# Values and gates of three row groups as seven half-block products

## Chip, cores and metric

The kernel runs on one core of a Trainium2 chip. The metric is the device time of one execution in microseconds; lower is better. The engines of the core that matter here are PE (TensorE, the matrix unit, with its weight loads shown as PEld), DVE (VectorE), ACT (ScalarE), POOL (GpSimd) and SP (SyncE, which here issues every DMA from one queue, in order).

## What is computed

The input x has 2048 rows of 1024 float32 values. It passes a retention layer and then a sliding-window attention layer; the change lies in the retention layer alone:

```python
def retention_layer(x, g_norm, w_in, w_out, sin, cos):
    proj = rmsnorm(x, g_norm) @ w_in            # 1024 -> 1024 + 1024 + 2048 + 2048
    q, k, v, gate = jnp.split(proj, [...])
    q = theta_shift(q.reshape(b, s, 4, 256), sin, cos)
    k = theta_shift(k.reshape(b, s, 4, 256), sin, cos)
    v = v.reshape(b, s, 4, 512)
    o = rms(retention(q, k, v))                 # chunks of 128 rows, a 256x512 state per head
    o = o.reshape(b, s, 2048) * silu(gate)
    return x + o @ w_out
```

Inside `retention` each chunk computes `scores @ v` plus `q @ state`, and then updates the state with `k.T @ v`.

## The kernel before

Rows are cut into 4 groups of 512 (`T`), and a group is worked through head by head: 4 groups x 4 heads give 16 units `u`, with `(g, h) = units[u]`. Every product in 32-bit precision is made of three fast ones: each operand is split into a rounded high part (`hi`, a cast on ACT) and the rest (`lo`, a subtraction on DVE), and PE computes hi-hi, hi-lo and lo-hi into the same PSUM bank.

For a unit, `main(u)` computes three projections with `proj` (L119): queries and keys together (L297), values (L325), gates (L332). Each goes over the 1024 inputs in 8 k-tiles of 128. `wload` (L100) fetches the weights in pieces of two k-tiles (128x1024, 512 KB) into one of three buffers of the tag `raw` (L105), casts them on ACT (L114) and subtracts on DVE (L116) into `whi` and `wlo`, three buffers each. A piece serves 24 matmuls (2 k-tiles x 4 PSUM banks x 3). The four banks come from the pool `pp`, which has four buffers in all, so the next projection writes a bank when the evacuation of the last one has read it. x is split once per group into `xhi`, `xlo` (L255, L256); the row scale of the norm is applied at the evacuation of values (L319, L320) and gates (L329). `row_stats` (L152) computes that scale.

`ret(u)` (L335) is the retention of one unit in four chunks; its PSUM banks come from another pool (`rr`, four buffers). The state `S32` stays in SBUF for each of the four heads. `out_a(u)` (L442) multiplies with the unit's rows of the output weights, again through `proj` (96 matmuls), and adds into the residual (L449). The order is laid down by the loop at L479: `drive` emits `main(u + 1)` and `ret(u)` interleaved, two steps of `main` per chunk, and then `out_a(u)`. A planner then orders each engine's instructions by priority and by its own estimate of when each is ready, so instructions of neighbouring steps mix; the retention has priority.

After the last unit, `prep_b0` (L438) loads the first x tiles of the second layer (phase B) while the last output projection runs; the last unit's output tiles `ohi`, `olo` take buffers of the x tiles (L350).

## Time and profile before

| | us |
|---|---|
| median of 3 runs (lowest, highest) | 2559.8 (2559.3, 2562.02) |
| profiled execution, its own time | 2558.99 |
| its span, first to last instruction | 2557.2 |
| PE busy | 2512.2 (98%) |
| DVE busy | 1495.7 (58%) |
| ACT busy | 1015.9 (40%) |

The busy time of an engine is the union of its instructions' times. PE's matmuls overlap each other in the pipeline, so the length of one matmul in the trace (about 0.39 us at 512 columns) is longer than the distance from one start to the next. The retention layer (phase A) covers about the first 1710 us of the span, the attention layer the rest.

### The profile page before, as it was taken

The page shows a single profiled execution, that of the slowest core. Times are in us where ns is not written, and L with a number is a line of the kernel's source. Part 1 is how long each engine was busy: PE and PEld are TensorE (multiplying, and loading weights), DVE is VectorE, ACT ScalarE, POOL GpSimd, SP SyncE. Part 2 cuts the span into 40 slices and gives each one's busy share as a digit, 9 for nine tenths or more (in the row PEclk, how much of TensorE's full clock was granted, in tenths as well). Part 3 has the DMA queues.
Part 4 walks back from the last instruction along what each step waited for, and adds up shares of the span by engine and source line. Part 5 has one row for each costly group of instructions (what it writes and reads, how often), then busy time and mean ns, then how long its engine had stood idle before and what let it go on. Part 6 is the DMA issues. An engine that isn't in the chain of part 4 may idle for free.

```text
span 2557.2 us, 31659 instructions
## 1 busy us (share of the span) xinstructions
PE 2512.2 (98%) x12098; PEld 2045.6 (80%) x12098; DVE 1495.7 (58%) x2653; ACT 1015.9 (40%) x1859; POOL 485.2 (19%) x429
## 2 busy tenths in 40 slices
PE   8999999999999999999999999989999999999998
PEld 7888888888888888888888888868777777777887
DVE  5445456454455554545545455467876677677766
ACT  4332333342333334223333332334544455454553
POOL 0000000110000021000011000041425454363360
PEclk9999999999999999999999999999999999999999
DMA  5242232422223243222323222237332352433333
GB/s 190 75 162 87 83 103 95 161 97 85 83 83 116 78 148 111 79 90 84 112 94 129 90 76 86 83 124 248 108 117 86 124 169 67 140 132 99 132 100 107
DMA packets 92501, 283.32 MB, mean 111 GB/s; under 512 B 11019, under 2 KB 17340, under 8 KB 92348
## 3 DMA queue, kind: packets, MB, share of 16 engines
q1 hardware_dynamic: 92348, 281.29, 32.9%
q8 instruction: 95, 1.56, 0.3%
q14 instruction: 58, 0.48, 0.1%
HBM read 245.58 MB, written 38.82 MB: 111 GB/s over the span
## 4 chain that ended last, share of the span: by engine, by line
PE 91%; DVE 4%; DMA 2%; issue 2%; ACT 1%; POOL 1%; SPq 0%; POOLq 0%; ACTq 0%; DVEq 0%
PE pp_ao L136 4%; PE pp_ao L138 4%; PE pp_ao L137 4%; PE o_t L670 2%; PE s_t L633 2%; PE pp_bo L136 2%; PE pp_bo L138 2%; PE pp_bo L137 2%; PE pT_t L654 2%; PE sc_r L356 1%; PE ot_r L427 1%; PE dl_r L393 1%; PE dl_r L394 1%; PE o_r L401 1%; PE o_r L403 1%
## 5 line engine op out<-in xcount | busy, mean ns | idle before, releaser
L94 POOL TENSOR_SCALAR r_o_r<-sso_r,es_a 128x1 f32<-128x1 f32 x64 | 31.2, 488 | 1260.3 <-ACT jo_r L421 1260.3
L136 PE MATMUL pp_ao<-ohi_r,whi_ao 128*128 128x512 f32 x512 | 203.3, 401 | 0.0
L137 PE MATMUL pp_ao<-olo_r,whi_ao 128*128 128x512 f32 x512 | 203.2, 397 | 0.0
L138 PE MATMUL pp_ao<-ohi_r,wlo_ao 128*128 128x512 f32 x512 | 199.5, 398 | 0.0
L116 DVE TENSOR_TENSOR wlo_ao<-raw_ao,whi_ao 128x1024 fp32r<-128x1024 f32 x64 | 78.4, 1224 | 199.7 <-ACT whi_ao L114 199.4
L644 ACT ACTIVATE P_t<-P_t,nm_t 128x256 f32<-128x256 f32 (+1 forms) x256 | 127.6, 499 | 143.6 <-DVE nm_t L636 142.9
L114 ACT CAST whi_ao<-raw_ao 128x1024 fp32r<-128x1024 f32 x64 | 67.1, 1048 | 184.9 <-PE pp_ao L137 49.6
L636 DVE CUSTOM_DVE_ANT_0 P_t<-s_t,bias,nsnk 128x256 f32<-128x256 f32 (+1 forms) x256 | 115.2, 469 | 34.8 <-PE s_t L633 34.0
L473 ACT CAST Shi_r<-S 128x512 fp32r<-128x512 f32 x120 | 70.3, 618 | 119.9 <-PE o_r L403 69.7
L137 PEld LDWEIGHTS pp_ao<-olo_r,whi_ao 128*128 128x128 f32 x512 | 96.9, 189 | 22.9 <-issue 0.2
L138 PEld LDWEIGHTS pp_ao<-ohi_r,wlo_ao 128*128 128x128 f32 x512 | 96.7, 189 | 23.0
L136 PEld LDWEIGHTS pp_ao<-ohi_r,whi_ao 128*128 128x128 f32 x512 | 96.8, 189 | 22.4 <-issue 0.2
L414 DVE SCALAR_TENSOR_TENSOR S<-S,dl_r 128x512 f32<-128x512 f32 x112 | 73.5, 682 | 65.5 <-PE dl_r L395 65.3
L633 PEld LDWEIGHTS s_t<-kst,qst_b 128*128 128x128 f32 x512 | 83.1, 193 | 30.6 <-DVE nm_t L636 7.6
L633 PE MATMUL s_t<-kst,qst_b 128*128 128x256 f32 (+1 forms) x512 | 101.1, 298 | 6.2 <-DVE nm_t L636 4.7
L474 DVE TENSOR_TENSOR Slo_r<-S,Shi_r 128x512 fp32r<-128x512 f32 x120 | 78.1, 686 | 38.7 <-ACT Shi_r L473 38.3
L650 DVE TENSOR_SCALAR P_t<-P_t,den_t 128x256 f32<-128x256 f32 (+1 forms) x256 | 99.4, 451 | 1.9
L136 PE MATMUL pp_bo<-ohi_t,whi_bo 128*128 128x512 f32 x224 | 89.0, 402 | 3.6 <-DVE gate_b L597 3.6
L137 PE MATMUL pp_bo<-olo_t,whi_bo 128*128 128x512 f32 x224 | 88.3, 394 | 0.0
L116 POOL TENSOR_TENSOR wlo_bo<-raw_bo,whi_bo 128x1024 fp32r<-128x1024 f32 x28 | 70.7, 2528 | 87.0 <-ACT whi_bo L114 64.8
L138 PE MATMUL pp_bo<-ohi_t,wlo_bo 128*128 128x512 f32 x224 | 86.3, 394 | 0.0
L424 DVE SCALAR_TENSOR_TENSOR gate_a<-o_r,r_o_r,gate_a 128x512 f32<-128x512 f32 x64 | 48.0, 750 | 55.0 <-POOL r_o_r L95 43.6
(867 smaller groups left out, 7292.0 us busy)
## 6 DMA issues: line engine op xcount, KB each, us to landing
raw_ao<-in_wo_a SPq DMA_DIRECT2D x64, 512.0 KB, 3.3
res<-xmid SPq DMA_DIRECT2D x56, 256.0 KB, 3.0
raw_bo<-in_wo_b SPq DMA_DIRECT2D x28, 512.0 KB, 3.3
xin<-in_x SPq DMA_DIRECT2D x16, 512.0 KB, 3.4
xraw_b<-xmid SPq DMA_DIRECT2D x16, 512.0 KB, 3.5
xmid<-res SPq DMA_DIRECT2D x32, 256.0 KB, 2.9
xraw_a<-in_x_t SPq DMA_DIRECT2D x12, 512.0 KB, 3.3
x_r<-in_x_t SPq DMA_DIRECT2D x12, 512.0 KB, 5.3
```

Of the source, the lines that this page charges most:

```text
L114: nc.scalar.copy(hi, raw)
L116: eng.tensor_tensor(lo, raw, hi.bitcast(F32), op=ALU.subtract)
L136: nc.tensor.matmul(o, hi[:, kk, sl], xh, start=st, stop=False)
L137: nc.tensor.matmul(o, hi[:, kk, sl], xl, start=False, stop=False)
L138: nc.tensor.matmul(o, lo[:, kk, sl], xh, start=False, stop=sp)
L414: nc.vector.scalar_tensor_tensor(S32[h][:, d, :], S32[h][:, d, :], gamC[h], dl[d], op0=ALU.mult, op1=ALU.add)
L473: nc.scalar.copy(hi, S32[h][:, d, :])
L474: nc.vector.tensor_tensor(lo, S32[h][:, d, :], hi.bitcast(F32), op=ALU.subtract)
L633: nc.tensor.matmul(o, qst[m][:, h, :], kst[:, kv * 2 + hl, kb + b0 : kb + 2, :], start=hl == 0, stop=hl == 1)
L636: nc.vector.tensor_tensor_reduce(out=pt[:, j, :w], in0=o, in1=bias[:, kv * GQ + h, b0 * P :], scale=-1.0, scalar=nsv[:, h : h + 1], op0=AL ...
L644: nc.scalar.activation(pt[:, j, :w], pt[:, j, :w], AF.Exp, scale=-1.0, bias=nm[:, c : c + 1], accum_out=den[:, c : c + 1])
L650: nc.vector.tensor_scalar_mul(pt[:, j, :w], pt[:, j, :w], den[:, c : c + 1])
```

## The change

For the row groups 1 to 3 (units 4 to 15; group 0 is `PLAIN`) values and gates are computed together as one product of 512 rows x 1024 inputs with 1024 x 1024 weights (values and gates side by side), cut into halves in each direction and computed by seven products of halves (256 rows x 512 inputs x 512 columns) in Winograd's form, where the direct way takes eight. It needs four sums of row halves (S1 to S4) and four sums of weight halves (T1 to T4). Both are computed on DVE from pieces loaded for that purpose and stored in DRAM: the weight sums in units 1, 3, 4 and 5 (one head each), the row sums and the scaled rows in units 2, 6 and 10 (for the next group), step by step through the list `behind`. The rows are scaled by the norm's row scale there, so no scale is applied to the gates at evacuation.

In `strassen`, products 0, 2, 4 and 5 accumulate in two banks of the tag `a`, one on top of the other; products 1, 3 and 6 in two banks of the tag `b`. ACT copies the sum in `a` out after products 0, 2 and 4, and DVE adds a bank of `b` to such a copy for three of the four quadrants. The next group's rows and sums are loaded from DRAM while the last head of a group runs its products (`after`). Every weight piece now serves 12 matmuls. The number of `main` steps per retention chunk goes from 2 to 3 in these units.

Queries and keys are loaded as separate pieces of four k-tiles of 256 columns. `q`, `k`, the key splits and several short tiles have one buffer, the state is stored to DRAM after each unit and loaded for the next head into one buffer, and the last unit's output tiles take buffers of the row sums. The DMA queue's scratch size is set to 1024.

The diff, cut to its core:

```diff
+RAW = 3
+PLAIN = 4
+SX = ("S2", "S3", "S1", "S4")
+ST = ("T2", "T3", "T1", "T4")
...
-    xtp = ctx.enter_context(tc.tile_pool(name="xtp", bufs=2))
+    xtp = ctx.enter_context(tc.tile_pool(name="xtp", bufs=1))
-    pp = ctx.enter_context(tc.tile_pool(name="pp", bufs=4, space=bass.MemoryType.PSUM))
+    pp = ctx.enter_context(tc.tile_pool(name="pp", bufs=2, space=bass.MemoryType.PSUM))
+    def pbank(tag, name):
+        return pp.tile([P, 512], F32, tag=tag, name=name)
...
     def xt_tiles(name):
+        return [[xtp.tile([P, 2, T], F32R, tag=f"x{hl}{j}", name=f"x{hl}_{name}_{j}") for j in range(4)]
+                for hl in ("hi", "lo")]
...
-        S32 = [cst.tile([P, 2, DV], F32, name=f"S{h}") for h in range(RH)]
+        S_d = [dram.tile([P, 2, DV], F32, name=f"Sd{h}") for h in range(RH)]
+        behind = []
+        def step():
+            if behind and next(behind[0], "end") == "end":
+                behind.pop(0)
+        def stp(name):
+            return p1.tile([P, T], F32, tag="st", bufs=6, name=name)
+        def short(name):
+            return p1.tile([P, 512], F32, tag="r", bufs=4, name=name)
...
+        def stage_rows(g):
+            for m in range(MT):
+                nc.vector.tensor_scalar_mul(dg[:, m * P : (m + 1) * P], ident, r[:, m : m + 1])
+            rp = bank(f"rpx_{g}")
+            nc.tensor.matmul(rp, ones, dg, start=True, stop=True)
+            nc.vector.tensor_copy(rb, rp)
+            yield
+            for k in range(KT // 2):
+                t = [stp(f"xst_{g}_{k}_{j}") for j in range(2)]
+                for j in range(2):
+                    kk = k + KT // 2 * j
+                    nc.sync.dma_start(t[j], x_t[g, kk // 2, :, kk % 2, :])
+                yield
+                for j in range(2):
+                    kk = k + KT // 2 * j
+                    nc.vector.scalar_tensor_tensor(t[j], t[j], ags[:, kk : kk + 1], rb, op0=ALU.mult, op1=ALU.mult)
+                a11, a21, a12, a22 = t[0][:, :H], t[0][:, H:], t[1][:, :H], t[1][:, H:]
+                nc.vector.tensor_tensor(s1, a21, a22, op=ALU.add)
+                nc.vector.tensor_tensor(s2, s1, a11, op=ALU.subtract)
+                nc.vector.tensor_tensor(s3, a11, a21, op=ALU.subtract)
+                nc.vector.tensor_tensor(s4, a12, s2, op=ALU.subtract)
+                for j in range(2):
+                    nc.sync.dma_start(d[kk // 2][:, kk % 2, :], t[j])
+                for n, v in zip(SX, (s2, s3, s1, s4)):
+                    nc.sync.dma_start(ds[n][:, k, :], v)
+                yield
+        def load_part(hi, lo, src, name):
+            raw = wp.tile(list(hi.shape), F32, tag="raw", bufs=RAW, name=f"xb_{name}")
+            nc.sync.dma_start(raw, src)
+            nc.scalar.copy(hi, raw)
+            nc.vector.tensor_tensor(lo, raw, hi.bitcast(F32), op=ALU.subtract)
...
+        def stage_sums(h):
+            for c in range(4):
+                b = [[stp(f"b{h}_{c}_{i}{j}") for j in range(2)] for i in range(2)]
+                for i in range(2):
+                    for j in range(2):
+                        nc.sync.dma_start(b[i][j], vg[i, j, c // 2, :, c % 2, :])
+                yield
+                nc.vector.tensor_tensor(b22, b22, b12, op=ALU.subtract)
+                nc.vector.tensor_tensor(b12, b12, b11, op=ALU.subtract)
+                nc.vector.tensor_tensor(b11, b22, b11, op=ALU.add)
+                nc.vector.tensor_tensor(b21, b21, b11, op=ALU.subtract)
+                for t, dt in zip((b11, b22, b12, b21), d):
+                    nc.sync.dma_start(dt[c // 2, :, c % 2, :], t)
+                yield
+        def strassen(n, src, xt, evac, after):
+            a = [pbank("a", f"pp_{n}a{f}") for f in range(2)]
+            def result(i, j, part=None, bk=None):
+                for f in range(2):
+                    if part is None:
+                        evac(i, j, f, a[f])
+                        continue
+                    nc.vector.tensor_tensor(r[part][f], r[part][f], bk[f], op=ALU.add)
+                    evac(i, j, f, r[part][f])
+            for p in range(7):
+                if p in (1, 3):
+                    b = [pbank("b", f"pp_{n}b{p}{f}") for f in range(2)]
+                dst = b if p in (1, 3, 6) else a
+                for i, w in enumerate(src(p)):
+                    hi, lo = wload(w, 512, f"{n}_{p}{i}")
+                    for kk in range(2):
...
+                        start, stop = k == 0 and p in (0, 1, 3), k == KT // 2 - 1
+                        for f in range(2):
+                            nc.tensor.matmul(dst[f], xh[:, sl], hi[:, kk, :], start=start, stop=False, **kw)
+                            nc.tensor.matmul(dst[f], xh[:, sl], lo[:, kk, :], start=False, stop=False, **kw)
+                            nc.tensor.matmul(dst[f], xl[:, sl], hi[:, kk, :], start=False, stop=stop, **kw)
+                    if i == 0:
+                        step()
+                        yield
+                if p in (0, 2, 4):
+                    r[p] = [short(f"r_{n}_{p}{f}") for f in range(2)]
+                    for f in range(2):
+                        nc.scalar.copy(r[p][f], a[f])
+                if p == 1:
+                    result(0, 0, 0, b)
+                elif p == 4:
+                    result(1, 1, 4, b)
+                elif p == 5:
+                    result(0, 1)
+                elif p == 6:
+                    result(1, 0, 2, b)
+                after(p)
+                step()
+                yield
...
-            q = p2.tile([P, 2, T], F32, tag="q", name=f"q_{n}")
-            k = p2.tile([P, 2, T], F32, tag="k", name=f"k_{n}")
+            q = p1.tile([P, 2, T], F32, tag="q", name=f"q_{n}")
+            k = p1.tile([P, 2, T], F32, tag="k", name=f"k_{n}")
...
+            yield from project_qk(u, xt, q, k, load_trig if u == 0 else None)
+            if plain:
+                yield from plain_vg(u, xt, put_v, put_gate)
+            else:
+                if h == 0:
+                    load_sums(g, SX[3])
...
+                def after(p):
+                    if h == RH - 1 and g + 1 < NG:
+                        if p in (1, 2, 6):
+                            for kp in {1: (0,), 2: (1,), 6: (2, 3)}[p]:
+                                load_rows(g + 1, kp)
+                        elif p:
+                            load_sums(g + 1, SX[p - 3])
+                yield from strassen(f"{n}v", src, xt, evac, after)
...
-                ohi, olo = (xtp.tile([P, 4, T], F32R, tag=f"x{hl}", name=f"o{hl}_{n}") for hl in ("hi", "lo"))
+                ohi, olo = ([xsp.tile([P, 2, T], F32R, tag=f"x{hl}S{i}", name=f"o{hl}{i}_{n}") for i in (2, 3)]
+                            for hl in ("hi", "lo"))
+            S32 = st.pop(("S32", u), None) or state_f32(u)
...
+            if g + 1 < NG:
+                nc.sync.dma_start(S_d[h], S32)
+            if u + 1 < nu and units[u + 1][0] > 0:
+                st["S32", u + 1] = state_f32(u + 1)
...
+            if u + 1 in (1, 3, 4, 5):
+                behind.append(stage_sums({1: 0, 3: 1, 4: 2, 5: 3}[u + 1]))
+            if h == 2 and g + 1 < NG:
+                behind.append(row_stats(g + 1))
+                behind.append(stage_rows(g + 1))
-            drive(tc, main(u + 1), ret(u), 2, 0)
-            for _ in itertools.islice(bias, 2):
+            drive(tc, main(u + 1), ret(u), 2 if u + 1 < PLAIN else 3, 0)
+            for _ in itertools.islice(bias, 2 if u >= RH else 0):
...
-    nc = _bacc.Bacc("TRN2", target_bir_lowering=False, num_devices=1)
+    nc = _bacc.Bacc("TRN2", target_bir_lowering=False, num_devices=1, dynamic_dma_scratch_size=1024)
```

## Rows read from the trace of the kernel before

**Rows 1.** The page: busy us of each engine, share of span, instructions
```profile
PE 2512.2 (98%) x12098; PEld 2045.6 (80%) x12098; DVE 1495.7 (58%) x2653; ACT 1015.9 (40%) x1859; POOL 485.2 (19%) x429
```
**Rows 2.** Stretches: length, busy us of each engine, clock, DMA share, GB/s
```profile
core 0: us, PE busy (x) PEld busy (x) DVE busy (x) ACT busy (x) POOL busy (x), PEclk, DMA share, GB/s
80.00:590.00 510.00, 510.00 (x2328) 419.48 (x2327) 265.19 (x342) 182.76 (x267) 44.37 (x69) 1.00 0.33 107
590.00:1018.00 428.00, 428.00 (x1951) 352.40 (x1949) 223.20 (x286) 149.44 (x216) 36.60 (x54) 1.00 0.31 102
1018.00:1440.00 422.00, 422.00 (x1925) 347.60 (x1924) 217.64 (x277) 144.58 (x205) 33.05 (x50) 1.00 0.29 97
1440.00:1640.00 200.00, 200.00 (x914) 164.80 (x913) 103.37 (x132) 63.88 (x91) 8.77 (x17) 1.00 0.25 82
1710.00:1730.00 20.00, 14.19 (x85) 13.15 (x84) 16.07 (x19) 8.82 (x11) 9.34 (x6) 0.83 0.69 248
1870.00:2500.00 630.00, 620.00 (x3318) 493.50 (x3317) 447.00 (x1102) 318.19 (x758) 286.98 (x168) 1.00 0.36 119
```
**Rows 3.** PE's waits over the span: total us, times, longest
```profile
PE pp_a0qk L136 <- ACT whi_a0qk L114: 7.3, 1, 7.3
PE pp_a0v L140 <- DVE th_a L291: 1.4, 1, 1.4
```
**Rows 4.** One tile's instructions (unit 7's gates): ns min/median/max, first and last start
```profile
L140 PEld LDWEIGHTS pp_a7g<-whi_a7g,xhi_a x32: 187/188/192, 773.2 to 794.2; 128*128 128x128 f32 x32
L140 PE MATMUL pp_a7g<-whi_a7g,xhi_a x32: 389/389/476, 773.2 to 794.4; 128*128 128x512 f32 x32
L142 PE MATMUL pp_a7g<-whi_a7g,xlo_a x32: 389/389/393, 773.8 to 794.9; 128*128 128x512 f32 x32
```
**Rows 5.** Groups by line and form: busy us, mean ns, idle before
```profile
L116 DVE TENSOR_TENSOR wlo_ao<-raw_ao,whi_ao 128x1024 fp32r<-128x1024 f32 x64 | 78.4, 1224 | 199.7 <-ACT whi_ao L114 199.4
L114 ACT CAST whi_ao<-raw_ao 128x1024 fp32r<-128x1024 f32 x64 | 67.1, 1048 | 184.9 <-PE pp_ao L137 49.6 <-issue 14.6 <-PE pp_a2g L142 8.8
L449 DVE TENSOR_TENSOR x_r<-x_r,pp_ao 128x512 f32<-128x512 f32 x96 | 65.4, 686 | 18.8 <-PE pp_ao L138 18.3
L429 ACT CAST ohi_r<-ot_r 128x512 fp32r<-128x512 f32 x64 | 37.3, 584 | 85.4 <-PE ot_r L427 85.2
L256 DVE SCALAR_TENSOR_TENSOR xlo_a<-xraw_a,ags,xhi_a 128x512 fp32r<-128x512 f32 x24 | 17.3, 748 | 17.8 <-ACT xhi_a L255 17.8
```
**Rows 6.** One tile's instructions: unit 7's raw gate weights
```profile
L114 ACT CAST whi_a7g<-raw_a7g x4: 1037/1052/1055, 756.7 to 779.5; 128x1024 fp32r<-128x1024 f32 x4
L116 DVE TENSOR_TENSOR wlo_a7g<-raw_a7g,whi_a7g x4: 1224/1226/1231, 757.8 to 780.6; 128x1024 fp32r<-128x1024 f32 x4
DMA to landing us min/median/max: 3.2/3.3/3.3
```
**Rows 7.** Single lines: a broadcast matmul, a 128x128 scaling, an SBUF subtraction
```profile
L179 PE MATMUL rp<-st,ones x2: 590/592/594, 1693.2 to 1693.7; 128*128 128x512 f32 x2
L177 DVE TENSOR_SCALAR st<-ident,r_b x4: 281/282/287, 1686.8 to 1687.4; 128x128 f32<-128x128 f32 x4
L294 DVE TENSOR_TENSOR q_a<-q_a,th_a x16: 678/680/682, 34.2 to 1589.8; 128x512 f32<-128x512 f32 x16
```
**Rows 8.** DMA queue and issues, 1725 to 1790 us; last line from the page
```profile
q1 hardware_dynamic: 6640, 16.20, 72.0%
raw_b0g<-in_w_b SPq DMA_DIRECT2D x4, 512.0 KB, 4.7
xmid<-x_r SPq DMA_DIRECT2D x12, 512.0 KB, 4.6
```
**Rows 9.** Timeline of SP and ACT around the layer's end: start, length
```profile
1705.22 0.33 SPq L106 DMA_DIRECT2D raw_b0kv<-in_w_kv  x1
1714.01 0.33 SPq L106 DMA_DIRECT2D raw_b0kv<-in_w_kv  x1
1713.40 1.98 ACT L192 CAST xhi_b<-xraw_b 128x1024 fp32r<-128x1024 f32 x2
```

More of the change, by code (lines that the diff above doesn't have):

```diff
@@ L120, in proj @@
         kn = 1024 // cols
-        bk = [pp.tile([P, 512], F32, tag="pp", name=f"pp_{name}_{m}") for m in range(4)]
+        bk = [pbank("ab"[m // 2], f"pp_{name}_{m}") for m in range(4)]
         for kp in range(nk // kn):
@@ L198, in out_proj @@
         for half in range(2):
-            yield from proj(src[half], 4, [ohi], [olo], True,
+            yield from proj(src[half], 4, ohi, olo, True,
                             lambda m, ps, half=half: evac(half * 4 + m, ps), f"{name}_{half}")
@@ L297, in main @@
-            yield from proj(w_a[h, 0], KT, xhi, xlo, True, evac_qk, f"{n}qk",
-                            before=load_first if u == 0 else None)
-            if u == 0:
-                for st["stats", 0] in row_stats(0):
-                    pass
-            ms, rx = st["stats", g]
-            ahead = row_stats(g + 1) if h == 1 and g + 1 < NG else None
-            def next_stats(kp):
-                st["stats", g + 1] = next(ahead)
+                if u:
+                    load_trig()
+            cs, sn = st["trig"]
@@ L325, in main @@
-            yield from proj(w_a[h, 1], KT, xhi, xlo, False, evac_v, f"{n}v", before=next_stats if ahead else None)
-            def evac_g(m, ps):
-                a = gp.tile([P, DV], F32, tag="gate", name=f"gate_{n}_{m}")
-                nc.scalar.activation(a, ps, AF.Silu, scale=rx[:, m : m + 1])
-                gate.append(a)
-            yield from proj(w_a[h, 2], KT, xhi, xlo, False, evac_g, f"{n}g")
-            st[u] = (q, k, vhi, vlo, gate, es)
+                if m == 0:
+                    ms, rx = st["stats", g]
+                    nc.gpsimd.tensor_tensor(vs, rx, rx, op=ALU.mult)
+                    nc.gpsimd.tensor_scalar(vs, vs, vd[:, h : h + 1], None, op0=ALU.mult)
+                    nc.gpsimd.tensor_scalar(es, ms, ep[:, h : h + 1], None, op0=ALU.mult)
@@ new lines, in evac_v, with before_v, before_g @@
+                put_v(m, ps, vs[:, m : m + 1])
+            def before_v(kp):
+                step()
+                if last:
+                    load_sums(1, SX[kp])
+            def before_g(kp):
+                step()
+                if last and kp:
+                    load_rows(1, kp - 1)
+            yield from proj(vg_pieces(h, 0), KT, xhi, xlo, False, evac_v, f"{n}v", before=before_v)
+            yield from proj(vg_pieces(h, 1), KT, xhi, xlo, False,
+                            lambda m, ps: put_gate(m, ps, st["stats", g][1][:, m : m + 1]), f"{n}g", before=before_g)
@@ L335, in ret, with vg_pieces @@
+            if last:
+                load_rows(1, 3)
+        def vg_pieces(h, j):
+            return [w_vg[h, kp // 2, j, kp % 2] for kp in range(KT // 2)]
         def ret(u):
```

315 lines of the change are left out of this document (190 added, 125 removed).

## Prediction

> **What bounds the kernel now.** I read four views in this order. The page's busy shares first: PE is busy for 98% of the span, DVE for 58%, ACT for 40% [rows 1]. A share over the whole span hides stages, so the stretches come next: from 80 to 1640 us, which is the retention layer without its first unit and its end, PE is busy in every microsecond of every stretch at full clock (510 of 510, 428 of 428, 422 of 422, 200 of 200), while DVE stands at 52%, ACT at 35% and the DMA engines at 31% in the 590 to 1018 us stretch [rows 2]. Third, PE's waits: over the whole span the longest is 7.3 us, the very first matmul on its first weights; the one wait at a join of two projections is 1.4 us, in the first unit [rows 3]. So until 1640 us nothing but the number of matmuls sets the pace. Fourth, the price of one matmul: the gate projection of one unit issues 96 of them (32 on each of three lines), first start 773.2, last start 794.9, so 21.7 us / 95 = 0.2284 us from start to start [rows 4]; the 0.389 us beside it is a latency, not a cost.
>
> The Trainium skill (Perfetto Trace Analysis, Identifying the Most-Contended Engine) says that matmul busy share doesn't show how near TensorE is to its limit, and that weight-load busy share does. By that measure PE stands at 352.4 / 428 = 82% in the main stretch [rows 2], which speaks against PE as the bound; it is weighed below as a rival.
>
> **The change, part by part.** All times are differences to the profiled execution, 2559.0 us (its span of 2557.2 and 1.8 around it); the median of the runs is 0.8 above it, which I ignore.
>
> *Fewer matmuls.* Before, values and gates of a unit are 2 projections x 8 k-tiles x 4 row tiles x 3 (hi-hi, hi-lo, lo-hi) = 192 matmuls. After, 7 products x 4 k-tiles x 2 row tiles x 3 = 168, of the same form (128x128 stationary, 512 columns moving). 24 fewer in each of 12 units: 288 x 0.2284 = **-65.8 us**, all on the path [rows 2 to 4].
>
> *A new broadcast of the row scale* for groups 1 to 3: one full-precision 512-column matmul each. The same form before starts its two passes 0.5 us apart [rows 7], so 1.0 us each: **+3**.
>
> *Weight feed.* Each product loads two 512 KB pieces and each piece now serves 12 matmuls, 12 x 0.2284 = 2.74 us, where it served 24 (5.48 us) before. 14 pieces instead of 8 per unit: 72 more casts on ACT at 1.05 us (76 us) and 72 more subtractions on DVE at 1.22 (88 us) [rows 5]. They lie beside PE if the three raw buffers turn fast enough. One turn is landing 3.3 us (quiet) to 4.7 (in a stretch with the DMA engines 72% busy), cast 1.05, subtraction 1.22 = 5.6 to 7.0 us [rows 5, 6, 8]; three pieces of matmuls last 8.2. So 1.2 to 2.6 us of queueing is covered per turn; if that cover goes, each microsecond more costs 1/3 us per piece. Expected cost 0 in an ordinary unit. In the last head of groups 1 and 2 eight further 512 KB tiles (the next group's rows and sums) pass through the same three buffers, mostly one per product: three turns in 5.48 us against 5.6 to 7.0, so 0.1 to 1.5 us short in each of six products and two units: 1 to 18 us. PE starts with pieces in hand and the shortage ends with the unit, so I take a value near the quiet landing: **+5**.
>
> *Accumulation in place.* Products 0, 2, 4, 5 add up in the same two PSUM banks, and ACT copies the sum out after 0, 2 and 4. After 0 and 2 a product on the other banks runs meanwhile (24 matmuls, 5.5 us, over two copies of 0.58 [rows 5]). After 4 nothing does: product 5 waits for the copy. The first bank is finished three matmuls (0.69 us) before the second, so the hole is about 0.58 + hand-over - 0.69, near 0, if ACT is free, and up to 1.05 more if a weight cast stands ahead of the copy. 0 to 12 us over 12 units; the scheduler may fill it with retention matmuls: **+4**. At the seam to the output projection its third bank needs two result additions (0.69 each [rows 5]) where six matmuls (1.4 us) give cover: 0 to 8, taken **+2**.
>
> *Results.* Three of four quadrants are added on DVE from PSUM: 6 x 0.686 x 12 = 49 us, and 6 x 0.584 x 12 = 42 us of copies on ACT [rows 5]; both beside PE.
>
> *Staging.* Weight sums: 4 heads x 4 x 4 subtractions of 128x512, SBUF to SBUF, at 0.68 = 44 us of DVE [rows 7]. Row sums, 3 groups x 4 steps of two scalings (0.748 [rows 5]) and four half-width operations: no such row exists; between the 128x128 scaling of 0.28 and the 128x512 of 0.68 [rows 7] I take 0.41, which gives 38 us. Reloading rows and sums in 24 tiles at 1.22 replaces 24 half tiles at 0.748: +11 [rows 5]. DVE so gains 88 + 49 + 44 + 38 + 11, with 5 for the scale's diagonal, 235 us in all. In group 1, which carries two heads' sums, 223 us in 428 becomes about 309 in 405: 76%. The sums come in bursts that sit ahead of a weight subtraction: 2.7 us per weight-sum step, 3.1 per row-sum step, against the 1.2 to 2.6 us of cover. Their loads, and stores that wait for DVE, stand on SP's queue ahead of weight loads. Only units 4 and 5 (weight sums) and 6 and 10 (row sums) do this at the doubled feed: 0 to 4 us each, taken **+4** together. Units 1 to 3 do it at 5.48 us per piece, where PE's buffers cover it.
>
> *Buffers kept once.* q, k, their splits and the state become single, and the state goes through DRAM after each unit: store and load of 512 KB one after the other, 4.6 + 3.3 us by the nearest transfers [rows 8, 6]. The load waits on SP for the store with weight loads queued behind it, but it falls at the end of a retention step, and the next one starts an output projection (96 x 0.2284 = 22 us) later: **0**, bounds 0 to +5. The last unit has no projection beside it, but it loads its state before.
>
> *Start.* x tiles and weights now share three raw buffers, and the key weights come as a second piece: the cover is the 5.5 us of the first piece's matmuls: **+1** (0 to 3).
>
> *End of the layer.* Before, the last unit's output tiles took the x buffers, so the second half of phase B's x tiles is cast only at 1713.4, after the last output matmul; the raw buffers they hold delay a weight load from 1705.2 to 1714.0 [rows 9], and PE has 5.8 idle us between 1710 and 1730 [rows 2]. After, these tiles go to the buffers of the sums. What is late next is the product with the norm weights on DVE: **-3** (-6 to +2).
>
> Sum: -65.8 + 3 + 5 + 4 + 2 + 4 + 0 + 1 - 3 = **-49.8**, so 2559.0 - 49.8 = **2509 us**.
>
> **The rivals.** *All cover holds*: only the matmul count, the broadcasts and up to 6 us at the end: 2559.0 - 65.8 + 3 - 6 = 2490 to 2496. For it: not one PE wait from 80 to 1640 us now [rows 2]. Against: what three raw buffers must keep up with shrinks from 16.4 to 8.2 us per turn.
>
> *DVE queueing shows everywhere*: at 76% busy, bursts delay casts and evacuations in most units. Phase B already runs so, DVE 447 of 630 us (71%), and PE idles 10 of 630 there, 1.6% [rows 2]; that rate over 12 units of 101 us is 19 us, about my stalls (15). If bursts also catch the feed, all four stall terms near their upper bounds give +30 to +45: 2530 to 2554.
>
> *The feed becomes the bound, slower than before*: if half of the 168 Strassen pieces meet a burst of two result additions, two value splits and two state operations on DVE (2 x 0.686 + 2 x 0.748 + 2 x 0.68 = 4.2 us [rows 5, 7]) at the loaded landing, a turn is 7.0 + 4.2 = 11.2 us, 3.73 per piece, 0.99 over the 2.74 of its matmuls: 84 x 0.99 = 83 us, against 62.8 saved: about 2579. It decides from 62.8 / 168 = 0.37 us lost per piece, that is turns of 9.3 us on average, 2.3 us more than a loaded landing without queueing. Against it: DVE's order is planned, and the bursts come per quadrant, not per piece.
>
> *PE isn't the bound*: were 18% of weight-load headroom real, something else would pace the stretch and the time would stay near 2559. That is the page's reading. But every matmul here has its own weight load, 188 ns in each 228 ns [rows 4]: 82% is the highest share that 512-column matmuls at this spacing allow. The trace disagrees with the page's rule here.
>
> **How the numbers follow.** The forecast, 2497 to 2530: 0.66. All cover holds: 0.10. DVE queueing, 2530 to 2554: 0.12. Within 0.2% of before (5 us, about what a measurement of this kernel can tell from no change; PE not the bound, or stalls that eat all): 0.04. Feed-bound and slower: 0.08. Faster 0.88, same 0.04, slower 0.08. The range that leaves out 2 in 10 takes in the upper part of the first rival and the lower half of the second: 2494 to 2540.
>
> **What would show it.** Right: 288 fewer matmuls on the value and gate lines, still 0.228 us apart inside a product; PE's waits from 80 to 1640 us at 10 to 20 us, the largest at product 5 on ACT's copy and in units 7 and 11 on weight casts; DVE about 1730 us busy in all; group 1 near 405 us long. Wrong: casts that wait for DMA or SP in ordinary units; a PE clock below full in a Strassen stretch; PE without waits (then 2494); or the layer's end later relative to its last output matmul.

## The result and the profile after

The changed kernel takes 2538.39 us (median; 2535.8 to 2541.82) against 2559.7: a ratio of 0.9916, 95% interval 0.9899 to 0.9933. The gain is 21.3 us. The forecast was 2509 us, 49.8 less than the profiled execution; the time lies inside the range given, but more than half of the gain is missing. By the profiled executions the span falls from 2557.2 to 2534.0, by 23.2, where the sum of the prediction had 49.8; the 26.6 us between are what the rest of this text looks for.

The page's engine line after, which answers to [rows 1]:

```profile
PE 2469.2 (97%) x11816; PEld 1996.7 (79%) x11816; DVE 1718.3 (68%) x2953; ACT 1128.5 (45%) x2008; POOL 476.7 (19%) x393
```

PE has 282 instructions fewer: 288 matmuls less and 6 more for the three broadcasts (two passes each). DVE's 1718 us are within 1% of the 1730 forecast. The work is what the prediction counted; the places where time is lost are not.

A table of the stretches shows where. Each number is worked out from the first start of one tile on PE to that of another (the tile views; `pp_aNqk` are the queries and keys of unit N, `pp_b0kv` is the first projection of the attention layer, `pp_b4kv` and `pp_b6kv` are the key-value projections of its row groups 2 and 3, `pp_l` is its last output projection). The forecast's sum is split the same way: 24 x 0.2284 = 5.5 us of gain per unit, 11 units between `pp_a4qk` and `pp_a15qk`.

| stretch | before | after | difference | forecast |
|---|---|---|---|---|
| start to `pp_a1qk` | 80.7 | 83.3 | +2.6 | +1 |
| to `pp_a4qk` (rest of group 0) | 315.3 | 325.1 | +9.8 | +1 |
| to `pp_a15qk` (groups 1 to 3) | 1163.9 | 1117.4 | -46.5 | -43.8 |
| to `pp_b0kv` (last unit, seam) | 152.6 | 143.7 | -8.9 | -8.0 |
| to `pp_l` (attention layer) | 806.8 | 826.5 | +19.7 | 0 |
| to the end | 37.9 | 38.0 | +0.1 | 0 |

So where the products are, the forecast held within 3 us; 10 us were lost in group 0, which has no such products, and 20 in the attention layer, which the change hardly names. The same in stretches (columns as in [rows 2]; the last one is the stretch of the attention layer 43 us earlier than there):

```profile
230.00:408.00 178.00, 171.31 (x769) 139.27 (x768) 119.69 (x167) 60.84 (x83) 7.20 (x13) 0.99 0.72 236
590.00:1018.00 428.00, 427.94 (x1932) 348.70 (x1931) 293.12 (x377) 194.73 (x278) 34.61 (x44) 1.00 0.54 176
1018.00:1440.00 422.00, 422.00 (x1911) 344.17 (x1910) 284.67 (x366) 187.39 (x264) 30.92 (x42) 1.00 0.49 161
1827.00:2457.00 630.00, 613.28 (x3229) 485.71 (x3227) 441.12 (x1074) 311.91 (x737) 276.75 (x164) 0.99 0.34 113
```

In groups 1 and 2 PE has no idle time, against 10 to 20 us forecast from 80 us on. At the end of group 0 it idles 6.7 us of 178 with the DMA engines 72% busy, and 16.7 of 630 in the attention layer, where it idled 10. Over the whole attention layer, from `pp_b0kv` to `pp_l`, first before, then after:

```profile
1712.50:2519.30 806.80, 783.41 (x4148) 621.93 (x4149) 592.06 (x1462) 411.17 (x979) 336.50 (x206) 0.99 0.39 131
1669.50:2496.00 826.50, 791.90 (x4148) 628.24 (x4149) 597.50 (x1461) 410.70 (x975) 333.69 (x204) 0.97 0.38 128
```

The matmuls are the same 4148. PE idles 34.6 us instead of 23.4, and it is busy 8.5 us longer, at a granted clock of 0.97 on average instead of 0.99. PE's longest waits after, (total, times, longest; answering to [rows 3]; that for the first weights and those at the layers' seam are left out):

```profile
PE s_t L867 <- DVE nm_t L870: 9.0, 7, 3.4
...
PE qtp_b L810 <- DVE qs_b L802: 7.4, 4, 3.2
PE pp_b6kv L147 <- DVE res L922: 3.5, 3, 2.0
...
PE pp_b4kv L147 <- DVE res L922: 2.3, 2, 1.3
PE pp_a3qk L483 <- DVE x_r L676: 2.2, 1, 2.2
...
PE pp_ao L143 <- DVE x_r L676: 2.1, 1, 2.1
PE pp_ao L143 <- ACT gate_a L415: 2.1, 1, 2.1
```

New against before, or longer, are the waits of `pp_b4kv` and `pp_b6kv` on a residual addition, those of group 0 (`pp_a3qk`, `pp_ao`), and the two at the top, which lie in the attention layer. The kernel before had:

```profile
PE s_t L633 <- DVE nm_t L636: 4.7, 5, 2.1
...
PE qtp_b L576 <- DVE qs_b L568: 3.9, 1, 3.9
...
PE pp_b6kv L140 <- DVE res L688: 0.4, 1, 0.4
```

One more thing is in no wait at all. Of neighbouring 512-column matmuls between 600 and 1000 us the starts lie 0.2311 us apart on average after and 0.2292 before (1503 and 1590 pairs). Over the some 4600 such matmuls between `pp_a4qk` and `pp_a15qk` that is 8.7 us.

### The profile page after: what moved, and what is told of

Its sections match the earlier page's. It is cut to its first block, busy times and chain, and to the rows that moved or that the text cites. A ratio compares the mean times of both kernels' runs of the same rounds, so it can differ in the third digit from the quotient of the medians.

```text
span 2534.0 us, 32377 instructions
## 1 busy us (share of the span) xinstructions
PE 2469.2 (97%) x11816; PEld 1996.7 (79%) x11816; DVE 1718.3 (68%) x2953; ACT 1128.5 (45%) x2008; POOL 476.7 (19%) x393
## 4 chain that ended last, share of the span: by engine, by line
PE 79%; DMA 9%; DVE 8%; ACT 2%; issue 1%; POOL 0%; SPq 0%; DVEq 0%; ACTq 0%
PE pp_ao L145 4%; PE pp_ao L143 4%; PE pp_ao L144 4%; PE o_t L904 2%; PE s_t L867 2%; PE pT_t L888 2%; PE pp_bo L143 1%; PE pp_bo L144 1%; PE pp_bo L145 1%; DMA res<-xmid 1%; DVE xlo_b L186 1%; PE o_r L613 1%; PE ot_r L640 1%; PE o_r L614 1%; PE o_r L612 1%
## 5 line engine op out<-in xcount | busy, mean ns | idle before, releaser
L101 POOL TENSOR_SCALAR r_o_r<-sso_r,ep 128x1 f32<-128x1 f32 x48 | 28.7, 597 | 920.8 <-ACT jo_r L634 920.8
L123 DVE TENSOR_TENSOR wlo_ao<-raw_ao,whi_ao 128x1024 fp32r<-128x1024 f32 x64 | 78.2, 1223 | 83.9 <-ACT whi_ao L121 83.8
L145 PEld LDWEIGHTS pp_ao<-ohi_r,wlo_ao 128*128 128x128 f32 x512 | 96.6, 189 | 24.6 <-DVE wlo_ao L123 1.2
L144 PEld LDWEIGHTS pp_ao<-olo_r,whi_ao 128*128 128x128 f32 x512 | 96.8, 189 | 23.2 <-issue 0.2
L701 DVE TENSOR_TENSOR Slo_r<-S,Shi_r 128x512 fp32r<-128x512 f32 x120 | 85.3, 736 | 37.8 <-ACT Shi_r L700 37.8
L676 DVE TENSOR_TENSOR x_r<-x_r,pp_ao 128x512 f32<-128x512 f32 x128 | 84.4, 683 | 17.9 <-PE pp_ao L145 17.2
```

Of the source, the lines that this page charges most:

```text
L123: eng.tensor_tensor(lo, raw, hi.bitcast(F32), op=ALU.subtract)
L144: nc.tensor.matmul(o, hi[:, kk, sl], xl, start=False, stop=False)
L145: nc.tensor.matmul(o, lo[:, kk, sl], xh, start=False, stop=sp)
L676: nc.vector.tensor_tensor(t, t, ps, op=ALU.add)
L701: nc.vector.tensor_tensor(lo, src[:, d, :], hi.bitcast(F32), op=ALU.subtract)
```

## Experiments

### The distance of matmuls: where the operands start

By the compiled program's memory plan the weights and x tiles of the retention layer start on a multiple of 64 bytes in each partition. The tiles laid out behind a few small constants (output tiles, state, and now the sums of the rows) start 32 bytes beyond one. After the change the values (`vhi`) start on a multiple too; before they didn't. The edit moves everything behind the constants by 32 bytes; the instructions and their order stay the same. It was made in the changed kernel (e1) and in the kernel before (e2):

```diff
-        ep = cst.tile([P, RH], F32, name="ep")
+        ep = cst.tile([P, 16], F32, name="ep")[:, :RH]
```

> The changed kernel with 32 bytes of padding behind one small constant, so that every tile of the retention layer starts 32 bytes later; instructions and their order are the same. Theory (the address): matmuls of 512 columns run 0.2333 us apart instead of 0.2268 when an operand starts 32 bytes off a multiple of 64. The sums' products (1152 matmuls) and the output projections (1536) fall to 0.227: 2688 x 0.0065 = 17 us, with the retention's own matmuls 18 to 22 us less than the changed kernel, about 2518. Rival (what else reads memory at the time: the doubled weight feed and the staging slow the reads): spacing stays at 0.231 on average, the time within 2 us of the changed kernel's 2538.

> The kernel before with the same 32 bytes. Theory (the address): output projections (1536 matmuls) go from 0.2333 to 0.227, some of the retention's too: 10 to 13 us less, 2547 to 2550. The value, gate and query projections, whose operands already start on 64, stay at 0.2265 to 0.228. Rival (other traffic): nothing, 2558 to 2561.

The third run pads the kernel before twice, so that weights and x tiles start 32 bytes off as well:

```diff
-    bgs = const.tile([P, KT], F32, name="bgs")
+    bgs = const.tile([P, 2 * KT], F32, name="bgs")[:, :KT]
...
-        ep = cst.tile([P, RH], F32, name="ep")
+        ep = cst.tile([P, 16], F32, name="ep")[:, :RH]
```

> The kernel before with two paddings: 32 bytes in front of all shared tiles and 32 more in front of those of the retention layer, so that in the retention layer every operand, weights and x tiles too, starts 32 bytes off a multiple of 64 (in the kernel before, only some do). Theory 1 (each operand for itself): all projections of that layer, 6 kinds alike, run 0.233 us apart, some 5000 matmuls x 0.006 = 30 us more than with one padding: 2570 to 2595. Theory 2 (the two operands against each other): what counts is that stationary and moving operand start differently; all start alike here, so every projection runs at 0.227 as with one padding, about 2546.

e1 took 2522.49 us (ratio to before 0.9847, 0.9832 to 0.9862). That is 18.3 us of span less than the changed kernel, but 15.9 by the medians, short of the 18 to 22 expected. e2 took 2548.16 (0.9952, 0.9935 to 0.9969), 13.3 us of span less than the kernel before and 11.5 by the medians; e10, a single run, took 2550.87. Mean distance of starts in us, 600 to 1000 us, worked out from the timelines:

| matmuls | before | e2, one padding | e10, two | after | e1, padding |
|---|---|---|---|---|---|
| output projection | 0.2332 | 0.2272 | 0.2271 | 0.2333 | 0.2270 |
| queries, keys | 0.2284 | 0.2268 | 0.2269 | 0.2276 | 0.2264 |
| values, or products in the banks `a` | 0.2280 | 0.2273 | 0.2275 | 0.2320 | 0.2279 |
| gates, or products in the banks `b` | 0.2270 | 0.2268 | 0.2270 | 0.2304 | 0.2272 |
| state update | 0.2312 | 0.2283 | 0.2278 | 0.2334 | 0.2314 |
| all | 0.2292 | 0.2272 | 0.2272 | 0.2311 | 0.2276 |

It can be read without averages where one unit's output projection runs uninterrupted, 96 matmuls. Its first and last start in the timeline of PE (start, length; us) of the kernel before, of e2 and of e10:

```profile
901.71 0.48 PE L136 MATMUL pp_ao<-ohi_r,whi_ao 128*128 128x512 f32 x1
...
923.95 0.40 PE L138 MATMUL pp_ao<-ohi_r,wlo_ao 128*128 128x512 f32 x1
```
```profile
894.95 0.48 PE L136 MATMUL pp_ao<-ohi_r,whi_ao 128*128 128x512 f32 x1
...
916.61 0.39 PE L138 MATMUL pp_ao<-ohi_r,wlo_ao 128*128 128x512 f32 x1
```
```profile
897.49 0.47 PE L136 MATMUL pp_ao<-ohi_r,whi_ao 128*128 128x512 f32 x1
...
919.13 0.39 PE L138 MATMUL pp_ao<-ohi_r,wlo_ao 128*128 128x512 f32 x1
```

22.24 us, 21.66 and 21.64: 0.2341, 0.2280 and 0.2278 per matmul. For the projections and the products the rival of other traffic falls, since the edit changed nothing else. In e10 the weights and the output tiles are both 32 bytes off, and the projection is as fast as with both on a multiple of 64; from `pp_a4qk` to `pp_a15qk` e10 and e2 both take 1153.5 us (e10's span is 5.2 us longer, outside that stretch). What counts here is that the two operands start alike, not where: theory 2 of e10. The misfit costs 0.006 us of 0.227. The state update does not follow this: by the memory plan both its operands stand 32 bytes off in the kernel before (0.2312) and in e10 (0.2278), and both on a multiple of 64 in e1 (0.2314); what else widens it was not traced. The misfit stood in the kernel before too (13.3 us), so of the 26.6 us that are missing it explains 18.3 - 13.3 = 5 by the spans, and 15.9 - 11.5 = 4.4 by the medians.

### The attention layer: quarters of x, and two residual buffers

Among the edits is that the x tiles are kept in quarters of two k-tiles instead of halves of four, in both layers. e3 puts the halves back, e7 makes the quarters the only edit of the kernel before, and e5 has halves and padding. The edit of e3:

```diff
-        return [[xtp.tile([P, 2, T], F32R, tag=f"x{hl}{j}", name=f"x{hl}_{name}_{j}") for j in range(4)]
-                for hl in ("hi", "lo")]
+        t = [[xtp.tile([P, 4, T], F32R, tag=f"x{hl}", bufs=2, name=f"x{hl}_{name}_{j}") for j in range(2)]
+             for hl in ("hi", "lo")]
+        return [[t[i][j // 2][:, j % 2 * 2 : j % 2 * 2 + 2, :] for j in range(4)] for i in range(2)]
```

> The changed kernel with the x tiles in halves of four k-tiles again (as in the kernel before) instead of quarters. It asks where the 20 us go that the attention layer took longer. Theory: the quarters let the next group's x tiles be loaded and split earlier, in front of the residual loads, and the key-value projections of groups 2 and 3 then wait for DVE; with halves they last 17 to 18 us again instead of 24 to 26, and the attention layer is 12 to 20 us shorter, about 2520 to 2526. Rival: the attention layer is longer for another reason (the single-buffered tiles, the smaller descriptor space of the DMAs): projections of 24 to 26 us again, the time within 4 us of 2538.

> The kernel before with only one edit of the change: x tiles in quarters instead of halves. Theory (the quarters alter the planned order in the attention layer): the attention layer, 806.8 us before, becomes 813 to 826 us, the retention layer stays as it was: 2565 to 2578 in all. Rival (something else of the change does it): 806 to 809 us, 2557 to 2562 in all.

> The changed kernel with both edits: the 32 bytes of padding and the x tiles in halves. Theory (two separate causes): the gains add up, 18 us from the addresses and 5 to 6 from the halves: some 2515 to 2518, the key-value projection of group 2 still 23 to 25 us long, that of group 3 18 us. Rival (the halves' gain was chance): the same as the padding alone, 2522.

The sixth run leaves the quarters and gives the residual tiles of the attention layer's output projection four buffers (on top of the padding):

```diff
-                t = p1.tile([P, T], F32, tag="res", bufs=2, name=f"res_{u}_{f}")
+                t = p1.tile([P, T], F32, tag="res", bufs=4, name=f"res_{u}_{f}")
```

> The changed kernel with the padding, and four buffers instead of two for the residual tiles of the attention layer's output projections. Theory (the queue): with two buffers the load of a residual tile stands on SP's queue behind two stores that wait for DVE, so the last residual additions come late and the key-value projections wait for their banks; with four, the projections of groups 2 and 3 last 17 to 19 us, PE has no wait on the residual addition there, and the attention layer, from the first key-value projection to the last output projection, falls from 822.6 to some 808 to 812 us: 2509 to 2513 in all. Rival (the planner's whole order of the attention layer is worse, whatever the buffers): still 818 us or more.

| | median | ratio to before | attention layer | `pp_b4kv` lasts | `pp_b6kv` lasts |
|---|---|---|---|---|---|
| before | 2559.7 | | 806.8 | 17.7 | 18.5 |
| after | 2538.39 | 0.9916 (0.9899 to 0.9933) | 826.5 | 24.6 | 26.7 |
| e7, quarters only | 2578.0 | one run | 818.0 | 25.0 | 24.8 |
| e3, halves | 2531.67 | 0.9891 (0.9872 to 0.9911) | 819.0 | 23.1 | 18.3 |
| e1, padding | 2522.49 | 0.9847 (0.9832 to 0.9862) | 822.6 | 24.6 | 25.5 |
| e5, halves and padding | 2515.65 | 0.9825 (0.9808 to 0.9842) | 818.1 | 23.3 | 18.7 |
| e6, padding and four buffers | 2502.63 | 0.9774 (0.9756 to 0.9792) | 805.3 | 17.1 | 17.6 |

(A projection lasts from its first to its last start on PE.) The quarters alone make the kernel before 17 us slower by its one run and 19.0 by the spans, 11.2 of it in the attention layer and 7.8 between the last unit and `pp_b0kv`. But putting the halves back takes only 4 to 8 us of 20 from the changed kernel: the theory of e3 holds for group 3's projection (`pp_b6kv`) and fails for group 2's (`pp_b4kv`), and the time misses its range of 2520 to 2526. What else in the change brings out the other 12 us was not taken apart. Four buffers take back all of it, more than e6 expected (808 to 812 us in the layer, 2509 to 2513 in all). So the two buffers are what makes the loss possible, and the quarters, with the rest of the new order, only bring it out. How that works is in four views of the changed kernel around `pp_b4kv`. SP's queue (start, time in the queue):

```profile
2056.66 3.95 SPq L923 DMA_DIRECT2D xmid<-res  x2
2060.70 3.93 SPq L921 DMA_DIRECT2D res<-xmid  x2
```

DVE:

```profile
2059.57 0.69 DVE L922 TENSOR_TENSOR res<-res,pp_bo 128x512 f32<-128x512 f32 x1 [2.63 <-DMA res<-xmid]
...
2064.89 0.69 DVE L922 TENSOR_TENSOR res<-res,pp_bo 128x512 f32<-128x512 f32 x1 [3.23 <-DMA res<-xmid]
```

PE:

```profile
2064.40 0.28 PE L147 MATMUL pp_b4kv<-whi_b4kv,xhi_b 128*128 128x256 f32 x1
2065.64 0.39 PE L147 MATMUL pp_b4kv<-whi_b4kv,xhi_b 128*128 128x256 f32 x1 [0.96 <-DVE res L922]
...
2067.68 0.39 PE L147 MATMUL pp_b4kv<-whi_b4kv,xhi_b 128*128 128x256 f32 x1 [1.31 <-DVE res L922]
...
2069.16 0.56 PE L149 MATMUL pp_b4kv<-whi_b4kv,xlo_b 128*128 128x256 f32 x1
2069.52 0.41 PE L148 MATMUL pp_b4kv<-wlo_b4kv,xhi_b 128*128 128x256 f32 x1
```

and the stretch around it:

```profile
2066.00:2075.00 9.00, 7.67 (x49) 7.01 (x48) 7.66 (x25) 4.12 (x14) 1.01 (x1) 0.81 0.71 244
```

A residual load stands in SP's queue behind the stores that free its buffer, which wait for DVE; DVE stands idle 3.23 us for the load, with the attention's own steps behind it; PE waits for the bank that the addition empties. PE idles only 2.3 us there, but the granted clock, 1.00 (2.4 GHz) before, is 0.81 on average in these 9 us, so in part at the lower level of 1.2 GHz: matmuls of 0.28 us stretch to 0.41 and 0.56. The same tile on PE in e6, where SP issues loads ahead of the stores that wait:

```profile
L147 PE MATMUL pp_b4kv<-whi_b4kv,xhi_b x32: 279/283/364, 2045.1 to 2061.9; 128*128 128x256 f32 x32
...
its engine sat idle before it (us, times) until:
who waited for it (us, times):
```

No wait is left, and 16.8 us from the first start to the last where the changed kernel needs 24.4. The granted clock stays up (e6, the same place, and then its whole attention layer, with 22.0 us of idle time on PE where the changed kernel has 34.6):

```profile
2050.00:2059.00 9.00, 9.00 (x73) 8.10 (x73) 5.68 (x25) 4.91 (x16) 2.39 (x1) 1.00 0.54 177
...
1657.60:2462.90 805.30, 783.30 (x4148) 622.54 (x4149) 591.30 (x1462) 408.87 (x975) 333.98 (x204) 0.98 0.39 131
```

In e5 the gains of halves and padding add up, as expected: 2515.65 is 6.8 us below e1.

### Group 0: the staging of the weight sums

e4 leaves out all staging, e8 only the weight sums; the products then read plain weights of the same size. Of e4, e8 and e13 to e15 there is one run each. The edit of e8:

```diff
-            if u + 1 in (1, 3, 4, 5):
-                behind.append(stage_sums({1: 0, 3: 1, 4: 2, 5: 3}[u + 1]))
...
-                    w = st["sums", h][name] if name else w_vg[(h,) + ((0, 0), (1, 0), 0, 0, 0, (1, 1))[p]]
+                    w = w_vg[(h,) + ((0, 0), (1, 0), (0, 1), (1, 1), (0, 0), (1, 1), (0, 1))[p]]
```

> The changed kernel without any staging of sums: no weight sums, no row scaling and no row sums are computed or stored; the products read plain weights and rows of the same size instead, so the result is not the layer's. Theory: the staging is what group 0 lost (its 12.4 us): the second group's first projection starts at 398 to 401 us instead of 408.4, the groups after it gain 1 to 4 us. Rival (the start and the buffers kept once cost it): the second group starts at 405 or later.

> The changed kernel without the sums of the weights (the products read plain weights in their place, so the result is not the layer's); the rows are still scaled, added and staged. Theory (bursts of 16 loads and stores and 16 DVE operations per head beside the plain units): the second group's first projection starts at 399 to 402 us, most of the way to the 397.8 without any staging. Rival (the rows' staging in the third and fourth unit costs it): 405 to 408 us. For the attention layer: its planned order here is nearer to that of the kernel before than that of any other variant, so if the order sets the length it is 807 to 815 us, and if the buffers do, 822 to 827.

The second group starts at 397.8 us in e4 and 399.1 in e8, against 408.4: the theory held, and the weight sums are nearly all of it. Their lack also frees the start (`pp_a1qk` at 78.2 and 78.7 instead of 83.3), so that this loss is no separate one. (e8's attention layer, 817.1 us, lies between the two ranges expected of it and decides nothing.) Which part of the staging does it? Two views of the changed kernel, DVE's waits from 275 to 310 us and PE's from 100 to 415 us (total, times, longest):

```profile
DVE b L326 <- DMA b<-in_w_vg: 8.6, 2, 4.4
DVE b L326 <- issue: 3.9, 1, 3.9
```
```profile
PE pp_a3qk L483 <- DVE x_r L676: 2.2, 1, 2.2
PE pp_ao L143 <- DVE x_r L676: 2.1, 1, 2.1
PE pp_ao L143 <- ACT gate_a L415: 2.1, 1, 2.1
```

DVE takes its instructions in order and stands at a sum whose pieces haven't landed; the residual addition that empties PE's bank is behind it. The timeline of DVE, then of PE, shows it at `pp_a3qk`:

```profile
299.24 0.69 DVE L326 TENSOR_TENSOR b<-b,b 128x512 f32<-128x512 f32 x1 [4.19 <-DMA b<-in_w_vg]
...
302.31 0.68 DVE L676 TENSOR_TENSOR x_r<-x_r,pp_ao 128x512 f32<-128x512 f32 x1
```
```profile
303.14 0.47 PE L483 MATMUL pp_a3qk<-xhi_a,whi_a3qk 128*128 128x512 f32 x1 [2.18 <-DVE x_r L676]
```

The third wait is of another kind. At 383.67 us PE waits for the evacuation of gates on ACT, and ACT had waited 8.2 and 4.8 us for two weight loads, the first of which stands on SP's queue behind four stores of sums; in e14 below, without stores, this wait is gone. Three runs tried to mend the waits of the additions on top of e6: the additions on POOL (e9), the additions one planning step later (e11), both (e12).

```diff
-                nc.vector.tensor_tensor(b22, b22, b12, op=ALU.subtract)
+                nc.gpsimd.tensor_tensor(b22, b22, b12, op=ALU.subtract)
...
                         nc.sync.dma_start(b[i][j], vg[i, j, c // 2, :, c % 2, :])
                 yield
+                yield
```

> The changed kernel with the padding, four residual buffers, and the additions of the weight sums on POOL instead of DVE (loads and stores stay on SP's queue). It asks by which way the weight staging holds PE up in the first group. Theory (DVE waits in order): DVE stands idle for the loads of the weight tiles, and the residual additions and splits behind it free PE's banks late; on POOL nobody waits for them, so the second group's first projection starts at 400 to 403 us instead of 409.8, and the whole is 2492 to 2496 us. Rival (SP's queue: the stores of the sums wait there with weight loads behind them, and POOL's additions, 1.6 us each against 0.7, make that longer): 409 us or later, 2502 or more.

> The changed kernel with the padding and four residual buffers; beside that, the DVE additions of the weight sums are put one planning step further behind the loads of their tiles, so that DVE shouldn't reach them before the data. Theory (DVE's in-order wait for the loads, 16.5 us in the first group): that wait falls below 8 us, and the first group loses less: the second group's second unit starts at 503 to 506 us instead of 509.2, 2496 to 2500 in all. Rival (the transfers themselves, with the DMA engines this busy, or the stores on SP's queue): the wait only moves to the weights, 508 us or later.

> The same with the additions on POOL. With them on POOL, PE waited 4.6 us on transposes of the retention's output, whose row scale on POOL stood behind the sums. Theory (an in-order wait that only moved from DVE to POOL): put behind the loads, the additions hold POOL 6.3 us a step and no longer for the loads; PE's wait there falls below 3 us and the second group's second unit starts at 500 to 503 us instead of 504.8; 2490 to 2496 in all. Rival (POOL's own time, not its waits, holds the row scale up): no change, 504 to 506 us.

e9 took 2499.39 us (0.9764, 0.9747 to 0.9781), e11 2498.85 (0.9767, 0.9752 to 0.9781), e12 2502.41 (0.9779, 0.9762 to 0.9795); e6 had 2502.63. `pp_a5qk`, at 509.2 in e6, starts at 504.8, 512.1 and 506.5 (`pp_a4qk`, which e9 was to bring to 400 to 403 us, starts at 409.6, 417.0 and 409.8, against 409.8 in e6; but up to 23 matmuls more of other steps lie ahead of it in the new orders, so it doesn't compare). All three theories missed by the place they named (e11's total alone fell into its range): the wait goes elsewhere. In e9 PE waits for the retention, whose row scale on POOL stands behind the sums, and DVE waits for it; first PE, then DVE:

```profile
PE ot_r L640 <- DVE gate_a L637: 4.6, 3, 2.8
```
```profile
DVE gate_a L637 <- POOL r_o_r L102: 12.0, 8, 5.8
```

In e11 DVE still waits 14.6 us for the pieces and PE 6.0 for the residual additions. So the parts were taken alone, in the changed kernel: the transfers without the additions (e13), loads and additions without the stores (e14), the additions over the first pieces alone (e15).

> The changed kernel with the loads and stores of the weight sums but without their additions on DVE (the tiles are stored as they were loaded, so the result is not the layer's). In the changed kernel the second group's second unit starts at 509.3 us, without any weight sums at 497.1. Theory T (the transfers: loads and stores on SP's queue and the busy DMA engines hold the weights up): still 506 to 510 us. Theory D (DVE, which waits in order for the tiles): 497 to 500 us.

> The changed kernel with the loads of the weight sums and their additions, but without the stores; the products read plain weights (the result is not the layer's). Theory T in the form that the stores on SP's queue do it (they wait there for DVE, with weight loads behind them): 497 to 501 us. Theory D: 506 to 510 us, as the waits of DVE for the loads stay; if the loads then come sooner, 501 to 505.

> The changed kernel with all 64 additions of the weight sums on DVE, but only the first quarter of the loads and no store (the additions run over the same four tiles again and again; the products read plain weights; the result is not the layer's). Theory D in the form of DVE's own time (2.7 us a step): 504 to 510 us. Theory T, or D in the form of waits for the loads: 497 to 501 us.

| | `pp_a4qk` | `pp_a5qk` | PE idle, 100 to 400 us |
|---|---|---|---|
| no weight sums (e8) | 399.1 | 497.1 | 0.0 |
| transfers alone (e13) | 398.9 | 496.9 | 0.0 |
| additions alone (e15) | 401.3 | 499.3 | 1.3 |
| loads and additions, no stores (e14) | 410.0 | 506.4 | 4.2 |
| all (after) | 408.4 | 509.3 | 6.7 |

The stretch from 100 to 400 us of e13 and of the changed kernel:

```profile
100.00:400.00 300.00, 300.00 (x1370) 246.52 (x1369) 175.79 (x236) 108.90 (x152) 18.99 (x30) 1.00 0.54 185
```
```profile
100.00:400.00 300.00, 293.31 (x1327) 239.68 (x1326) 186.14 (x257) 104.48 (x148) 15.63 (x28) 0.99 0.56 182
```

With the same 0.54 to 0.56 of the DMA engines' time, e13 loses nothing: the transfers alone are not the cause. The rest is read at `pp_a5qk`, ahead of which each of the five has started the same 2210 matmuls. The stretch up to there in e8 and in the changed kernel:

```profile
0.00:497.10 497.10, 488.66 (x2210) 401.09 (x2211) 283.07 (x367) 192.06 (x265) 34.83 (x59) 1.00 0.43 143
```
```profile
0.00:509.30 509.30, 491.62 (x2210) 401.25 (x2211) 312.03 (x418) 191.11 (x264) 34.58 (x59) 1.00 0.57 191
```

Of the 12.2 us 9.2 are idle time of PE; in the other 3.0 PE is busy longer with the same matmuls. The additions alone cost 2 us. Additions that wait for their loads cost 9, and the stores, which wait for the additions, 3 more. Single executions of the same instructions scatter by 3 us at the start (`pp_a1qk` at 80.7, 81.0 and 83.6 in the kernel before, e2 and e10), so the 2 and the 3 are not clear of that; the 9 and the 12 are. It is the coupling on an in-order engine.

## Why the prediction was right and wrong

**Right.** The count of matmuls, DVE's load and the single prices: result additions 0.683 us (0.686 taken), value splits 0.744 (0.748), additions of the weight sums 0.69 (0.68), half-width row sums 0.417 (0.41, bounded by the nearest rows). The end of the layer: -8.9 with the last unit's 5.5, so about -3.4 for the -3. The rival that PE isn't the bound, which the prediction drew from the Trainium skill (Perfetto Trace Analysis, Identifying the Most-Contended Engine), fell. With the weight loads at 348.7 of 427.9 us, 81% (82% before), the stretch shortened by what the matmul count says, less the terms below.

**Right only in sum: groups 1 to 3.** The stalls (+14.5 of the 15 fall here) did not come. Product 5's wait for ACT's copy, the seam, the feed in units 7 and 11 and the bursts in units 4 to 10 together show, beside the broadcasts, two distances over 0.40 us in 1117 us, and PE idles 0.1 us there. Each of these terms had 0 as its lower bound, and 0 is what came: the rival that all cover holds, given 0.10, is what happened where the products are. That PE had work of other steps to fill each hole, as the prediction itself said of product 5, is argued from the missing waits. In their place came 8.7 us of wider spacing, more than half of it from operands that start 32 bytes apart. The prediction held the 0.2284 us of one projection for every matmul of that form; [rows 4] is a projection whose operands start alike (0.2277 by the timeline's 773.24 and 794.87), and the output projections of the same trace, 0.2332, were not looked at. With the misfit gone in both kernels (e1 against e2) this stretch gains 1153.5 - 1102.4 = 51.1 us of the 58.3 that 264 matmuls less two broadcasts are worth; some 2 of the rest are spacing (0.2276 against 0.2272), and 2 to 3 are 9 matmuls of the retention and 2 of the attention's bias that the new order starts inside the stretch (249 matmuls fewer there, not 260); the remaining 2 to 3 were not traced.

**Wrong: staging in units 1 to 3 costs nothing.** The step "at 5.48 us per piece, where PE's buffers cover it" looked at weights only. Against the transfers the weights were covered, as e13 shows; not covered was the residual addition behind a DVE that waits for the pieces of a sum, and, by 2.1 us, weight loads behind stores that wait for DVE. The price is 10 to 12 us, with the +1 for the start among it.

**Wrong: the attention layer wasn't in the sum.** The x tiles in quarters stood in the diff; the prediction gave them no term, since they add no instruction. They alter the order that the planner lays down (e7: 11.2 us in this layer from the quarters alone) in a layer with two residual buffers and no slack; by which step they alter it was not traced. The price of the whole new order was 19.7 us, and e6 shows the missing slack as the cause. The second rival, DVE queueing (2530 to 2554), holds the time that came, but for a place where nothing was lost.

**Luck.** That the time lies between 2494 and 2540 is luck: the upper part of that range stood for DVE queueing beside the products, where nothing was lost, and the losses outside the sum happened to be of that size.

Together: 19.7 us in the attention layer, 10.4 in group 0 and the start and 0.1 at the end, less 2.7 and 0.9 where it went better than forecast, are the missing 26.6 us.

**What beats both kernels.** The changed kernel with the 32 bytes and four residual buffers, 2502.63 us, is 2.3% below before and 1.4% below the change. The kernel before gains from the 32 bytes too (e2), and against that the distance is 1.8%; what four buffers would give it was not run. With the sums on POOL or later it is 2499, which these runs don't tell from 2502.63.

## What to carry to other kernels

Price an edit also where it only alters which buffer is free when: name the stretches that are planned anew, and for each the in-order queue with a load, the instruction waiting for it, and what stands behind; a buffer more there can be worth more than the arithmetic saved. Before counting matmuls at one price, compare the spacing of every kind of them in the trace, and where two kinds of one shape differ, look at where their operands start. And compare the stretches that a change does not touch: here the largest loss lay in one of them.

## What was not expected of the hardware

In the output projections here, matmuls of 128x512 with a 128x128 stationary operand start 0.227 to 0.228 us apart when both operands start on a multiple of 64 bytes, or both 32 bytes off one, and 0.233 to 0.234 apart when one does and the other doesn't (22.24 against 21.66 and 21.64 us for 96 of them). The state update, of the same form, does not keep to this. 32 bytes of padding were worth 13.3 us of the span of the kernel before and 18.3 of the changed one. And a wait of PE can cost more than its length: after 2.3 us of waits at `pp_b4kv` the granted clock was 0.81 over 9 us, where it stayed 1.00 in the same place without the waits; over the attention layer PE was busy 8.5 us longer with the same matmuls, beside its 11.2 us more of idle time.
